# A hybrid recurrent decoder step on one core: zeros by ScalarE, VectorE's PSUM copies, one engine per bank in the planner, and a split start of the DeltaNet projection

## The chip, the core and the metric

The kernel runs on one core of a Trainium2 chip. The core has five instruction streams: TensorE (PE in the profile, PEld for its weight loads), VectorE (DVE), ScalarE (ACT), GpSimd (POOL) and SyncE (SP), which here only issues DMAs. The metric is the device time of one execution in microseconds.

## The reference

One step of a four-layer decoder trunk runs for a prompt of 256 tokens and for a sample group of 8 sequences with 4 new tokens each. That makes 288 token columns, all in fp32 with D_MODEL = 1024. Layers 0 and 3 use an S5 mixer, layer 1 an RG-LRU, layer 2 a gated DeltaNet. A causal ConvFFN follows each.

```python
def rmsnorm(x, g):
    return x * lax.rsqrt(jnp.mean(x * x, axis=-1, keepdims=True) + RMS_EPS) * g

def s5_mixer(x, h0_re, h0_im, w_in, a_re, a_im, log_dt, b_re, b_im, c_re, c_im, d, w_glu):
    u = x @ w_in
    lam = lax.complex(a_re, a_im);  dt = jnp.exp(log_dt)[:, None]
    a_bar = jnp.exp(lam * dt)
    b_bar = ((a_bar - 1.0) / lam)[..., None] * lax.complex(b_re, b_im)
    ...            # h[t] = a_bar * h[t-1] + b_bar u[t], y = Re(c h), in 64 groups of 16 channels
    y = jax.nn.gelu(y + d * u)
    val, gate = jnp.split(y @ w_glu, 2, axis=-1)
    return val * jax.nn.sigmoid(gate), h_last

for i in range(4):
    h = rmsnorm(x, mixer_gain[i]);  x = x + mixer[i % 3](h)
    h = rmsnorm(x, ffn_gain[i])
    up, conv = causal_dwconv(h @ w_up[i]);  x = x + (silu(gate half) * value half) @ w_down[i]
y = rmsnorm(x, final_gain)
```

The DeltaNet projects h to queries, keys, values, gates z and 16 scalars (beta and decay for 8 heads), convolves q, k and v, and runs a chunked delta rule. All recurrent states are returned too.

## The kernel before

The residual x stays in SBUF, transposed: 8 blocks of 128 channels by 288 tokens. Each projection is tiled into output tiles of 128 channels. A tile is summed over its k-blocks in one PSUM bank (names ps or px).

**Two ways to multiply.** In the split form the weight unit wr (128x1024, loaded by a DMA on SP's queue) is cut into a rounded part wh (ScalarE) and a rest wl (VectorE or GpSimd). The operand is cut likewise into xh and xl. Each k-block then takes three products of the type fp32r: xh·wh, xl·wh and xh·wl. In the whole form there is no cut, and each k-block is one plain fp32 product, which the trace shows as two records. `whole(u)` (L493) says which unit takes which: before, all of s5_in and gdn_in and a part of lru_in are whole. `WHOLE` lists the norms whose operand xh is written in plain fp32; the others write xh and xl.

**The planner.** The kernel is written as generators, which a small scheduler runs in Python when the program is built (class `Net`, with `tick`, `spawn`, `after`, `mark`). Each engine's wrapper (class `Eng`) books a price for every instruction, and `Trace.free` says from when its operands may be touched. The order that comes out of this is fixed in the program. A generator spawned with a lower rank goes first. All instructions are emitted by one wrapper line (L235 before, L243 after), so that rows are told apart by tile names.

**The stages in order.** s5_in, s5_glu, FFN 0, lru_in, lru_out, FFN 1, gdn_in, gdn_out, FFN 2, s5_in, s5_glu, FFN 3, final norm. Each begins when the residuals (x) before it are summed.

**The S5 layer** (`s5`, L1179). For each of 8 blocks m of 8 groups, `prep` (L1280) builds the state's input weights. TensorE writes them to a bank through vx and ci, VectorE scales 32 columns into wt, and 96 columns are copied to wt by whichever engine the planner thinks is free. `chain` (L1367) then takes the two-bank product pv, multiplies it by the phase tables e_r and e_i on VectorE (x, y), copies the sample part to fin on ScalarE, writes the decay tile r4 on ScalarE with a zero column by GpSimd, scans on VectorE (x<-r,x), builds the chunk states ss (its first columns copied from h0 on GpSimd, a column of the end state copied to fin on GpSimd) and forms the output y. vx and ca are block-diagonal tiles; their zeros are written once per layer by GpSimd. The tables (`s5_tables`, L1027: ex, er, dt, ang, rho, ...) are small VectorE operations on 32 columns. For layer 3 they run within FFN 2, as its `beside`.

**The end** (`final`, L2274). Eight squares are summed over channels by products with a column of ones. rsqrt is a chain of 11 VectorE operations on 128x3. The result is spread over a diagonal (dg), broadcast by a product with ones (busy), copied to SBUF (rstd), and eight operations write y, each with a DMA of its own.

Fills: when the planner thinks that TensorE would idle, it emits products on a constant tile (busy) into a warm bank.

Of the kernel before, what the change touches and what calls it, by code (L numbers as in the profile page):

```python
# [16 lines left out]
P = 128  # L17
D = 1024
# [19 lines left out]
OE, CE = 0, 'a'  # L38
PRS, DB, TH, BI = 1, 4, 8, 0.0
SR, SS = (0, 2, 1), (1000.0, 2000.0)  # L40
WHOLE = (0, 4, 6)
# [62 lines left out]
class Trace:  # L104
# [11 lines left out]
    def free(self, kind, writes, reads):  # L116

        at = 0.0
        for ts, w in ((writes, True), (reads, False)):
            for t in ts:  # L120
                a, b, c, d = self.region(t)
                for (e, f, g, h), wrote, by, end in self.tiles.get(self.place.get(t.name, t.name), ()):
                    if (w or wrote) and end + SEEN[by][kind] > at and a < f and e < b and c < h and g < d:
                        at = end + SEEN[by][kind]
        return at
# [21 lines left out]
class Eng:  # L147
# [56 lines left out]
    def __getattr__(self, name):  # L204
        f = getattr(self.real, name)

        def call(*a, **k):
            out = k["out"] if "out" in k else a[0]
            n = math.prod(out.shape[1:])
            args = [b for b in (*a, *k.values()) if hasattr(b, "ap")]  # L210
            writes = [b for b in args if b is out or b is k.get("accum_out")]
            reads = [b for b in args if not any(b is w for w in writes)]
            free = self.net.trace.free(self.kind, writes, reads)
            if self.kind == "pe":
                end = self.product(name, a[1], a[2], k.get("tile_position"), free)
            else:
                fn = a[2] if len(a) > 2 else None
                if self.kind == "a" and any(fn in s for s in SETS) and fn not in self.table:

                    self.t += 1283.0  # L220
                    self.table = next(s for s in SETS if fn in s)
                c = self.price(n, name)
                if self.kind in "va" and n > 1 and any(math.prod(b.shape[1:]) == 1 for b in reads):
                    c += self.POINTER[self.kind]
                streams = sum(b.space != PSUM and math.prod(b.shape[1:]) > 1 for b in reads)
                shared = self.kind == "g" and streams > 0 or self.kind == "v" and (
                    streams > 1 or streams == 1 and name in SINGLE and out.space != PSUM
                )
# [64 lines left out]
class Net:  # L293
# [121 lines left out]
    def tick(self):  # L415
        self.ahead()
        while self.warm and self.pe.cool():

            bank, alone = self.warm[-1]
# [52 lines left out]

    def scale(self, out, in_, s, kinds="va"):
# [243 lines left out]
    def ffn(self, li, gi, beside=()):  # L717
# [5 lines left out]
        with ExitStack() as es:  # L723
# [455 lines left out]
    def s5(self, li, gi, tables=None):  # L1179
# [7 lines left out]
        with ExitStack() as es:  # L1187
# [33 lines left out]
            def doubles():  # L1221
# [4 lines left out]
                self.warm.insert(0, (big[0][:, 1], True))  # L1226
# [3 lines left out]
                del self.warm[0]  # L1230
# [23 lines left out]
            for _, v in vxs.free + cas.free:  # L1254
                G.memset(v, 0.0)
# [24 lines left out]
            def prep(m):  # L1280
# [34 lines left out]
                self.copy(w[:, :96], ps[:, :96])  # L1315
# [51 lines left out]
            def chain(m, ps):  # L1367
# [24 lines left out]
                A.activation(fin[:, :, q0:q1, :NB], pv[:, :, :, :NB], AF.Copy)  # L1392
# [20 lines left out]
                G.tensor_copy(ssm[:, :, :, 0:NB], h0[:, :, q0:q1, :])  # L1413
# [7 lines left out]
                G.tensor_copy(fin[:, :, q0:q1, NB], ssm[:, :, :, NCK])  # L1421
# [83 lines left out]
            G.memset(cas.free[-1][1], 0.0)  # L1505
# [23 lines left out]
    def gdn(self, gi):  # L1529
# [6 lines left out]
        with ExitStack() as es:  # L1536
# [61 lines left out]

            def scalars():
                yield from self.after("gw")  # L1600
                ps = yield from self.banks.get()
                for k in range(KD):
                    yield from self.after(("x", g0, k))
                    PE.matmul(ps[0:16, :T], wab[:, k, :], self.xh[:, k, :], start=k == 0, stop=k == KD - 1)
                    if k % 2:
                        yield PE
                yield
# [633 lines left out]
            for m, ps in zip(tiles, self.gemm("gdn_in", tiles[:start], KD, self.xh, self.xl, self.xready(g0))):  # L2241
                self.spawn(fns[m // NH](m % NH, ps), rank=rk(m))
            for m in tiles[start:]:
                self.spawn(fns[m // NH](m % NH, *self.gemm("gdn_in", [m], KD, self.xh, self.xl)), rank=rk(m))
# [29 lines left out]
    def final(self):  # L2274
        self.drain()
        self.spawn(self.norm_rstd(8))
        self.drain()
        yp = self.ctx.enter_context(self.tc.tile_pool(name="yp", bufs=4))
        for m in range(KD):
            y = yp.tile([P, T], F32, name="y", tag="y")  # L2280
            self.v.scalar_tensor_tensor(
                y, self.x[:, m, :], self.gains[:, 8, m : m + 1], self.rstd, op0=ALU.mult, op1=ALU.mult
            )
            self.dma(self.o["y"][:, m, :], y)
# [192 lines left out]
```

## Time and profile before

| | us |
|---|---|
| three runs | 1572.19, 1572.41, 1567.34; median 1572.19 |
| the profiled execution, its own time | 1569.18 |
| its span | 1567.4 |
| PE / DVE / ACT / POOL busy in the span | 1503.2 / 1280.4 / 807.0 / 360.8 |
| s5_in, s5_glu (layer 0) | 7.1 to 184.1 |
| FFN 0 | 184.1 to 396.0 |
| gdn_in | 728.8 to 937.1 |
| FFN 2's down projection | 1110.9 to 1184.9 |
| s5_in, s5_glu (layer 3) | 1184.9 to 1340.7 |
| final norm and y | 1552.2 to 1567.4 |

TensorE is busy for 96% of the span, so the stages in which it is not are of interest. [...] A timeline row gives the start, the busy time, the engine and the operation, and in brackets how long the engine had been idle and what released it. Starts tell the pace of TensorE, since products overlap.

### The profile page before, as it was taken

The page shows a single profiled execution, that of the slowest core. Times are in us where ns is not written, and L with a number is a line of the kernel's source. Part 1 is how long each engine was busy: PE and PEld are TensorE (multiplying, and loading weights), DVE is VectorE, ACT ScalarE, POOL GpSimd, SP SyncE. Part 2 cuts the span into 40 slices and gives each one's busy share as a digit, 9 for nine tenths or more (in the row PEclk, how much of TensorE's full clock was granted, in tenths as well). Part 3 has the DMA queues.
Part 4 walks back from the last instruction along what each step waited for, and adds up shares of the span by engine and source line. Part 5 has one row for each costly group of instructions (what it writes and reads, how often), then busy time and mean ns, then how long its engine had stood idle before and what let it go on. Part 6 is the DMA issues. An engine that isn't in the chain of part 4 may idle for free. (4 is left out here: it accounts for less than half of the span.)

```text
span 1567.4 us, 32702 instructions
## 1 busy us (share of the span) xinstructions
PE 1503.2 (96%) x12527; PEld 1390.6 (89%) x12527; DVE 1280.4 (82%) x2884; ACT 807.0 (51%) x1594; POOL 360.8 (23%) x734
## 2 busy tenths in 40 slices
PE   6689999999999999999999999999999899999996
PEld 5568999999988999998777779999997779999996
DVE  8898799975868899943887677999997967899944
ACT  3475466654574566642543334666444635566631
POOL 2021044520211245400111010444201310245400
PEclk8799999999999999999999999999999999999998
DMA  4422444455425544554322536544545235544552
GB/s 156 113 88 87 161 177 162 163 174 172 174 81 152 195 168 164 163 174 149 122 95 70 195 101 212 178 171 161 156 149 157 55 105 169 166 169 163 161 176 68
DMA packets 84909, 230.05 MB, mean 147 GB/s; under 512 B 19088, under 2 KB 28688, under 8 KB 84752
## 3 DMA queue, kind: packets, MB, share of 16 engines
q1 hardware_dynamic: 84752, 227.96, 44.5%
q8 instruction: 98, 1.61, 0.4%
q14 instruction: 59, 0.48, 0.1%
HBM read 216.94 MB, written 10.99 MB: 145 GB/s over the span
## 5 line engine op out<-in xcount | busy, mean ns | idle before, releaser
L235 DVE TENSOR_TENSOR wl<-wr,wh 128x1024 fp32r<-128x1024 f32 (+2 forms) x338 | 397.9, 1179 | 132.1 <-PE px L235 36.5
L235 ACT ACTIVATE wh<-wr 128x1024 fp32r<-128x1024 f32 (+2 forms) x338 | 344.9, 1023 | 208.2 <-PE ps L235 77.7
L235 DVE SCALAR_TENSOR_TENSOR cv<-ext,par,cv 128x304 f32<-128x304 f32 (+1 forms) x420 | 258.2, 615 | 11.3 <-ACT cv L235 3.3
L235 PE MATMUL px<-xh,wh 128*128 128x288 f32 x776 | 231.0, 298 | 0.0
L235 PE MATMUL px<-xl,wh 128*128 128x288 f32 x776 | 228.9, 295 | 0.0
L235 PE MATMUL px<-xh,wl 128*128 128x288 f32 x776 | 228.7, 295 | 0.0
L235 PE MATMUL ps<-xh,wh 128*128 128x288 f32 x712 | 210.6, 296 | 0.0
L235 PE MATMUL ps<-xl,wh 128*128 128x288 f32 x712 | 210.0, 295 | 0.0
L235 PE MATMUL ps<-xh,wl 128*128 128x288 f32 x712 | 209.9, 295 | 0.0
L235 POOL TENSOR_TENSOR pr<-cv,cv 128x32 f32<-128x32 f32 (+1 forms) x156 | 165.9, 1083 | 58.8 <-DVE cv L235 55.3
L235 POOL COPY sto<-ext 128x16 f32<-128x16 f32 (+3 forms) x379 | 103.4, 275 | 310.8 <-DVE ext L235 287.2
L235 ACT ACTIVATE cv<-ext,par 128x304 f32<-128x304 f32 (+1 forms) x210 | 130.6, 626 | 85.1 <-DVE ext L235 70.7
L235 PE MATMUL ps<-gl,wh 128*128 128x288 f32 x568 | 169.7, 299 | 3.6 <-DVE gl L235 3.3
L235 PE MATMUL ps<-gh,wh 128*128 128x288 f32 x568 | 169.5, 298 | 2.6 <-ACT gh L235 2.5
L235 PE MATMUL ps<-gh,wl 128*128 128x288 f32 x568 | 169.0, 298 | 0.3 <-DVE wl L235 0.3
L235 PE MATMUL px<-gh,wh 128*128 128x288 f32 x536 | 159.1, 297 | 2.4 <-DVE gh L235 2.4
L235 PE MATMUL px<-gh,wl 128*128 128x288 f32 x536 | 158.8, 296 | 0.3 <-DVE wl L235 0.3
L235 PE MATMUL px<-gl,wh 128*128 128x288 f32 x536 | 159.0, 297 | 0.0
L235 PEld LDWEIGHTS px<-xh,wh 128*128 128x128 f32 x776 | 145.9, 188 | 0.8
L235 PEld LDWEIGHTS px<-xl,wh 128*128 128x128 f32 x776 | 145.9, 188 | 0.8
L235 PEld LDWEIGHTS px<-xh,wl 128*128 128x128 f32 x776 | 145.8, 188 | 0.0
L235 PE MATMUL ps<-xh,wr 128*128 128x288 f32 x416 | 125.4, 436 | 12.1 <-DMA wr<-s_in 7.1
(547 smaller groups left out, 3055.0 us busy)
## 6 DMA issues: line engine op xcount, KB each, us to landing
wr<-ffn_up SPq DMA_DIRECT2D x176, 512.0 KB, 3.5
wr<-ffn_down SPq DMA_DIRECT2D x64, 448.0 KB, 3.3
wr<-s_glu SPq DMA_DIRECT2D x32, 512.0 KB, 3.9
wr<-ffn_down SPq DMA_DIRECT2D x32, 512.0 KB, 3.5
wr<-gdn_in SPq DMA_DIRECT2D x32, 512.0 KB, 3.5
wr<-lru_in SPq DMA_DIRECT2D x20, 512.0 KB, 3.2
wr<-s_in SPq DMA_DIRECT2D x16, 512.0 KB, 3.8
wr<-lru_out SPq DMA_DIRECT2D x16, 320.0 KB, 2.9
```

The source lines that it names most:

```text
L235: return f(*a, **k)
```

## The change

1. **DeltaNet projection.** The first eight tiles (the keys, `NP3 = 8`) and the 16 scalars take the split form; the norm before it therefore writes xh and xl. From the ninth tile on the whole form is used as before, on a plain fp32 operand xf that ScalarE writes anew into the buffer of xl (`operand`).
2. **FFN 2.** The tables of layer 3 are spawned after the first down tile, at rank 1, in place of ahead of it.
3. **The final norm.** Sums over squares go into three banks, the earlier blocks' before the last is there, with fills between. The reciprocal root is broadcast by three fp32 products against the identity, y is read straight from PSUM and written to one tile, and five DMAs take it out in place of eight.
4. **S5.** Zeros of vx, ca and sx come from ScalarE. The 96 columns of wt and the sample part fin are copied by VectorE alone. r4's zero column is written once per buffer, outside the loop. The copies ss<-h0 and fin<-ss go from GpSimd to ScalarE. Two warm banks are offered in place of one.
[...]

```diff
-WHOLE = (0, 4, 6)
+WHOLE = (0, 6)
+RB = 1
+NP3 = 8
+NK = 4, 10
@@ Trace.free
-                    if (w or wrote) and end + SEEN[by][kind] > at and a < f and e < b and c < h and g < d:
+                    late = end + SEEN[by][kind]
+                    if t.space == PSUM and by != kind:
+                        if late > at and c // 512 <= (h - 1) // 512 and g // 512 <= (d - 1) // 512:
+                            at = late
+                    elif (w or wrote) and late > at and a < f and e < b and c < h and g < d:
@@ Eng
-                shared = self.kind == "g" and streams > 0 or ...
+                shared = self.kind == "g" and (streams > 0 or name == "memset") or ...
@@ Net
+    def zero(self, t):
+        ...
+        self.act.activation(t, a.to_broadcast(list(t.shape)), AF.Copy, scale=0.0)
@@ whole
-        return name.startswith(("s5_in", "gdn_in")) or name == "lru_in" and m >= KL
+        return name.startswith("s5_in") or name == "gdn_in" and m >= NP3 or name == "lru_in" and m >= KL
@@ ffn
-            for g in beside:
-                self.spawn(g)
...
                 if m == 0:
                     self.dma(self.o["ffn_st"][li], sto)
+                    for g in beside:
+                        self.spawn(g, rank=RB)
@@ s5
             for _, v in vxs.free + cas.free:
-                G.memset(v, 0.0)
+                self.zero(v.rearrange("p i q t c -> p (i q t c)"))
+            for _, r in r4s.free:
+                G.memset(r[:, :, :, 0], 0.0)
...
-                self.copy(w[:, :96], ps[:, :96])
+                V.tensor_copy(w[:, :96], ps[:, :96])
...
-                A.activation(fin[:, :, q0:q1, :NB], pv[:, :, :, :NB], AF.Copy)
+                V.tensor_copy(fin[:, :, q0:q1, :NB], pv[:, :, :, :NB])
...
-                A.activation(r4, s.rho4[:, q0:q1].unsqueeze(1).unsqueeze(3).to_broadcast(X), AF.Copy)
-                yield
-                G.memset(r4[:, :, :, 0], 0.0)
+                A.activation(r4[:, :, :, 1:], rho.to_broadcast([P, 2, 4, NP - 1]), AF.Copy)
...
-                G.tensor_copy(ssm[:, :, :, 0:NB], h0[:, :, q0:q1, :])
+                self.copy(ssm[:, :, :, 0:NB], h0[:, :, q0:q1, :], CE)
...
-                G.tensor_copy(fin[:, :, q0:q1, NB], ssm[:, :, :, NCK])
+                self.copy(fin[:, :, q0:q1, NB], ssm[:, :, :, NCK], CE)
@@ gdn
+                for k in range(KD):
+                    for i, (w, x) in enumerate(((wah, self.xh), (wah, self.xl), (wal, self.xh))):
+                        PE.matmul(ps[0:16, :T], w[:, k, :], x[:, k, :], ...)
...
+                if m == NP3:
+                    while not self.marked("gx"):
+                        self.idle()
+                    x2 = self.xs.tile([P, KD, T], F32, name="xf", tag="xl"), None
+                    self.spawn(operand(x2[0]), rank=-1)
@@ final
+            for i, b in enumerate((*BLK[:2], slice(0, NS))):
+                PE.matmul(ps[:, b], r[:, i : i + 1].to_broadcast([P, P]), self.ident[:, :n], start=True, stop=True)
+            for m in range(KD):
+                V.scalar_tensor_tensor(
+                    y[:, m, :], self.x[:, m, :], self.gains[:, 8, m : m + 1], ps[:, :T], op0=ALU.mult, op1=ALU.mult
+                )
+                if m not in (2, 4, 6):
+                    self.dma(self.o["y"][:, e : m + 1, :], y[:, e : m + 1, :])
```

**TensorE at the start of gdn_in**, before: the first tile sums in ps_72, the scalars (wab) in px_1686, the second tile in ps_73; `dg,busy` broadcasts the norm's reciprocal root.

```order
L235 MATMUL px_1685<-busy,sm_96 128x1
L235 MATMUL ps_72<-xh,wr 128x288 x4
L235 MATMUL px_1686<-xh,wab 16x288 x2
L235 MATMUL ps_73<-xh,wr 128x288
...
L235 MATMUL ps_75<-dg,busy 128x288
```

The same place after, with the scalars in ps_72 and the tile in px_1718:

```order
L243 MATMUL ps_72<-xh,wh 16x288
L243 MATMUL ps_72<-xl,wh 16x288
L243 MATMUL ps_72<-xh,wl 16x288
...
L243 MATMUL px_1718<-xh,wh 128x288
L243 MATMUL px_1718<-xl,wh 128x288
L243 MATMUL px_1718<-xh,wl 128x288
L243 MATMUL ps_74<-dg,busy 128x288
```

Each whole product on xh and wr has become a triple on xh, xl, wh and wl; the norm's broadcast keeps its place.

**VectorE at the start of FFN 2's down projection**, before: cuts wl of the coming weights, the tables (er, dt) and the gate's rest gl, which the last k-block of the first down tile needs.

```order
L235 SCALAR_TENSOR_TENSOR er<-ek,ex 128x32
L235 SCALAR_TENSOR_TENSOR er<-ek,er 128x32
L235 TENSOR_SCALAR dt<-er 128x32
L235 SCALAR_TENSOR_TENSOR cv_10713<-ext_10711,par,cv_10713 128x304 x2
L235 TENSOR_TENSOR wl<-wr,wh 128x896
L235 SCALAR_TENSOR_TENSOR dt<-dt,er 128x32 x7
L235 SCALAR_TENSOR_TENSOR dt<-dt,es 128x32
L235 TENSOR_TENSOR gl<-pr_10719,gh 128x288
```

The same place after:

```order
L243 SCALAR_TENSOR_TENSOR cv_10918<-ext_10916,par,cv_10918 128x304 x2
L243 TENSOR_TENSOR wl<-wr,wh 128x896
L243 TENSOR_TENSOR pr_10924<-cv_10917,cv_10918 128x32
L243 TENSOR_TENSOR pr_10924<-cv_10917,cv_10918 128x256
L243 CAST gh<-pr_10924 128x288
L243 TENSOR_TENSOR gl<-pr_10924,gh 128x288
L243 TENSOR_TENSOR wl<-wr,wh 128x1024
L243 TENSOR_TENSOR x<-x,px_1718 128x288
L243 TENSOR_SCALAR ex<-sc 128x32
```

The tables (ex and what follows) now stand behind the last gate and the first residual, and the last gate product pr and its cast gh are VectorE's too.

**ScalarE in s5_in of layer 0**, before, from the first chain on:

```order
L235 ACTIVATE vx_145<-pa_162 64x16x16 x4
L235 ACTIVATE fin<-px_634 128x2x4x8
L235 ACTIVATE r_172<-rho_107 128x512
L235 ACTIVATE ci_137<-ci_137 128x128
L235 ACTIVATE wt_141<-px_635 128x96
L235 ACTIVATE wh<-wr 128x1024
```

The same place after, and what follows when the first chunk states are there:

```order
L243 ACTIVATE vx_145<-pa_162 64x16x16 x4
L243 ACTIVATE r_172<-rho_107 128x8x63
L243 ACTIVATE ci_137<-ci_137 128x128
L243 ACTIVATE wh<-wr 128x1024
...
L243 ACTIVATE ss_146<-h_127 128x8x8
L243 ACTIVATE vx_144<-pa_164 64x16x16 x4
L243 ACTIVATE fin<-ss_146 128x2x4
L243 ACTIVATE r_172<-rho_107 128x8x63
L243 ACTIVATE ci_136<-ci_136 128x128
```

fin<-px and wt no longer stand in ScalarE's row ahead of ci; fin<-ss, which waits for VectorE's ss, does later on.

## Rows read from the trace of the kernel before

**Rows 1.** Windows by stage: stretch, length, busy PE, PEld, DVE, ACT, POOL, clock, DMA.

```profile
659.00:728.80 69.80, 69.80 (x530) 69.80 (x529) 34.37 (x47) 28.75 (x40) 2.40 (x4) 1.00 0.54 167
728.80:937.10 208.30, 206.43 (x1875) 153.66 (x1873) 158.79 (x506) 86.32 (x283) 23.58 (x61) 1.00 0.37 121
1110.90:1184.90 74.00, 72.20 (x530) 71.56 (x530) 67.31 (x211) 28.87 (x41) 4.11 (x7) 0.98 0.52 157
```

**Rows 2.** Timeline of PE in gdn_in: start, busy time, operation, count.

```profile
918.55 2.11 PE L235 MATMUL px<-xh,wr 128*128 128x288 f32 x8
920.49 2.10 PE L235 MATMUL ps<-xh,wr 128*128 128x288 f32 x8
```

**Rows 3.** Groups by form in gdn_in: operation, count, busy time, mean ns of one.

```profile
L235 ACT ACTIVATE wh<-wr 128x1024 fp32r<-128x1024 f32 x4 | 4.2, 1058 | 2.0 <-DMA wr<-gdn_out 2.0
L235 DVE TENSOR_TENSOR wl<-wr,wh 128x1024 fp32r<-128x1024 f32 x2 | 2.5, 1225 | 1.6 <-ACT wh L235 1.6
```

**Rows 4.** Timeline of PE, first down tile of FFN 2.

```profile
1120.36 0.40 PE L235 MATMUL ps<-gh,wh 128*128 128x288 f32 x1 [0.90 <-ACT gh L235]
1121.66 0.40 PE L235 MATMUL ps<-gl,wh 128*128 128x288 f32 x1 [0.90 <-DVE gl L235]
```

**Rows 5.** Timeline of DVE at the same place.

```profile
1118.94 2.07 DVE L235 SCALAR_TENSOR_TENSOR dt<-dt,er 128x32 f32<-128x32 f32 x7
```

**Rows 6.** Window of PE alone behind that: length, busy PE, clock, DMA.

```profile
1122.00:1126.50 4.50, 4.50 (x25) 0.62 0.58 191
```

**Rows 7.** Timeline of DVE in the final norm.

```profile
1556.91 0.42 DVE L235 TENSOR_TENSOR dg<-ident,rsr 128x256 f32<-128x256 f32 x1
...
1559.48 1.80 DVE L235 SCALAR_TENSOR_TENSOR y<-x,gains,rstd 128x288 f32<-128x288 f32 x4
...
1561.92 2.03 DVE L235 SCALAR_TENSOR_TENSOR y<-x,gains,rstd 128x288 f32<-128x288 f32 x4 [0.64 <-DMA o_y<-y]
```

**Rows 8.** Windows of the S5 layers up to the last gate, columns as in rows 1.

```profile
5.36:141.10 135.74, 109.90 (x1335) 86.61 (x1335) 121.17 (x348) 64.53 (x152) 21.29 (x38) 0.87 0.31 97
1184.90:1297.20 112.30, 102.40 (x1352) 82.06 (x1350) 88.26 (x182) 56.92 (x133) 22.92 (x42) 0.95 0.32 95
```

**Rows 9.** Timeline of the start: POOL, DVE, ACT.

```profile
3.17 1.85 POOL L235 MEMSET ca<- 128x1024 f32 x2
...
2.46 2.90 DVE L235 TENSOR_SCALAR ex<-sc 128x32 f32<-128x32 f32 x1 [2.46 <-DMA sc<-s_sc]
...
5.72 0.44 ACT L235 ACTIVATE acc<-x 128x288 f32<-128x288 f32 x1 [3.70 <-DMA x<-x]
```

**Rows 10.** Timeline in s5_in of layer 0: ACT, PE, DVE.

```profile
68.18 0.22 ACT L235 ACTIVATE fin<-px 128x64 f32<-128x64 f32 x1 [4.10 <-DVE x L235]
...
69.31 1.10 PE L235 MATMUL px<-vx,ci 128*32 128x128 f32 x14 [5.03 <-ACT ci L235]
...
76.17 1.29 DVE L235 TENSOR_TENSOR x<-px,ee 128x512 f32<-128x512 f32 x2 [3.46 <-PE px L235]
```

**Rows 11.** The tile wt, both layers: durations min/median/max in ns, and who waited for it (us, times).

```profile
L235 ACT ACTIVATE wt<-px x4: 251/252/253, 36.5 to 1211.4; 128x96 f32<-128x96 f32 x4
...
L235 DVE COPY wt<-px x2: 249/250/250, 89.7 to 1257.3; 128x96 f32<-128x96 f32 x2
...
  ACT wt L235: 23.5, 9
```

**Rows 12.** The tile fin, both layers: what its writers' engines waited for (us, times).

```profile
  DVE x L235: 41.1, 15
  DVE ss L235: 29.1, 11
```

**Rows 13.** Timeline in s5_in of layer 3: POOL, PE.

```profile
1238.78 5.48 POOL L235 COPY ss<-h 128x64 f32<-128x64 f32 x1
...
1244.31 0.46 PE L235 MATMUL px<-ss,ca 128*32 128x72 f32 x16 [2.19 <-DVE wt L235]
```

**Rows 14.** Window behind it, columns as in rows 1.

```profile
1245.90:1252.70 6.80, 6.80 (x68) 6.21 (x57) 5.55 (x10) 4.82 (x11) 2.95 (x4) 0.50 0.01 4
```

More of the change, by code (lines that the diff above doesn't have):

```diff
@@ L417, in tick @@
         while self.warm and self.pe.cool():
-            bank, alone = self.warm[-1]
+            at = [w for w in self.warm if self.trace.free("pe", [w[0]], []) <= self.now]
+            if not at:
+                break
+            bank, alone = at[-1]
             self.pe.matmul(
@@ L471, in tt @@
         self.best(math.prod(out.shape[1:])).tensor_tensor(out, a, b, op=op)
+    def zero(self, t):
+        n = len(t.shape) - 1
+        a = self.ident[:, :1]
+        for _ in range(n - 1):
+            a = a.unsqueeze(2)
+        self.act.activation(t, a.to_broadcast(list(t.shape)), AF.Copy, scale=0.0)
     def scale(self, out, in_, s, kinds="va"):
@@ L1225, in doubles @@
                 twos.put(*big)
-                self.warm.insert(0, (big[0][:, 1], True))
+                self.warm[:0] = [(big[0][:, i], True) for i in range(2)]
                 self.banks.put(*small)
@@ L1229, in doubles @@
                 yield from twos.get(PRS)
-                del self.warm[0]
+                del self.warm[:2]
                 if small:
@@ L1504, in s5 @@
             vts.free.append((0.0, more[:, 1024:2048].rearrange("p (q i n) -> p q i n", q=4, i=2)))
-            G.memset(cas.free[-1][1], 0.0)
+            self.zero(more[:, :1024])
             while not self.marked(*(("sv", li, m) for m in range(GW))):
@@ L1597, in pack, with operand @@
                     V.tensor_copy(pk[32 * h : 32 * h + 32, dst, :], src[0:32, 2, h::4])
+            def operand(xf):
+                for m in range(KD):
+                    A.activation(xf[:, m, :], self.x[:, m, :], AF.Copy, scale=self.gains[:, g0, m : m + 1])
+                    self.mark(("xf", m))
+                    if m % 2:
+                        yield
+                self.mark("xf")
             def scalars():
                 yield from self.after("gw")
+                wah, wal = (w.rearrange("p (k c) -> p k c", k=KD) for w in (wh, wl))
+                self.copy(wah, wab)
+                yield
+                V.tensor_tensor(wal, wab, f32(wah), op=ALU.subtract)
+                yield
                 ps = yield from self.banks.get()
@@ L1603, in scalars @@
                     yield from self.after(("x", g0, k))
-                    PE.matmul(ps[0:16, :T], wab[:, k, :], self.xh[:, k, :], start=k == 0, stop=k == KD - 1)
+                    for i, (w, x) in enumerate(((wah, self.xh), (wah, self.xl), (wal, self.xh))):
+                        PE.matmul(ps[0:16, :T], w[:, k, :], x[:, k, :], start=k + i == 0, stop=k == KD - 1 and i == 2)
                     if k % 2:
                         yield PE
+                self.mark("gx")
                 yield
@@ L2274, in final, with norm @@
     def final(self):
-        self.drain()
[L2276 to L2284, printed above, removed]
+        V, PE = self.v, self.pe
+        y = self.xs.tile([P, KD, T], F32, name="y", tag="xh")
+        def norm():
+            yield from self.after(("n", 8, KD - 2))
+            pss = yield from self.banks.get(3)
+            spare = yield from self.banks.get()
+            for m in (KD - 2, KD - 1):
+                yield from self.after(("n", 8, m))
+                for ps, b in zip(pss, BLK):
+                    sq = self.acc if m < KD - 1 else self.last
+                    PE.matmul(ps[:, :1], sq[:, b], self.ones[:, :1], start=m < KD - 1, stop=m == KD - 1)
+                for _ in range(NK[m - KD + 2]):
+                    PE.matmul(
+                        spare[:, : 2 * P].rearrange("p (a c) -> p a c", a=2), self.busy,
+                        self.busy.unsqueeze(1).to_broadcast([P, 2, P]), start=True, stop=True,
+                    )
+            v = self.work.tile([P, 3], F32, name="nv", tag="nv")
+            for i, ps in enumerate(pss):
+                V.tensor_scalar(v[:, i : i + 1], ps[:, :1], 1.0 / D, EPS, op0=ALU.mult, op1=ALU.add)
+            r = self.rsqrt(v, [P, 3], "nr")
+            ps = pss[0]
+            for i, b in enumerate((*BLK[:2], slice(0, NS))):
+                n = b.stop - b.start
+                PE.matmul(ps[:, b], r[:, i : i + 1].to_broadcast([P, P]), self.ident[:, :n], start=True, stop=True)
+            e = 0
+            for m in range(KD):
+                V.scalar_tensor_tensor(
+                    y[:, m, :], self.x[:, m, :], self.gains[:, 8, m : m + 1], ps[:, :T], op0=ALU.mult, op1=ALU.mult
+                )
+                if m not in (2, 4, 6):
+                    self.dma(self.o["y"][:, e : m + 1, :], y[:, e : m + 1, :])
+                    e = m + 1
+        self.spawn(norm())
+        self.drain()
 def wtiles(w):
```

9 lines of the change are left out of this document (6 added, 3 removed).

## The prediction

> **What bounds the kernel now.** I read the windows by stage first. The FFN stages have TensorE busy for their whole length: the down projection of FFN 1 takes 69.80 us with 69.80 of PE [rows 1]. Nothing can be gained there but by fewer products. Its 528 products give the pace of the split form: 69.80 / 528 = 0.1322 us. The DeltaNet projection is bound by TensorE too: 206.43 of 208.30 us busy, with VectorE at 158.79 [rows 1]. There the form of the products sets the time. The down projection of FFN 2 has the same products as that of FFN 1 and takes 74.00 us, 4.2 more, with VectorE at 67.31 in place of 34.37 [rows 1]. The timelines then tell of the rest. The S5 layers are the two places where TensorE waits for the other engines. Up to the last gate, VectorE is busy for 121.17 of 135.74 us in layer 0, and for 88.26 of 112.30 in layer 3 [rows 8]. So layer 0 is nearly VectorE's length, and layer 3 is a chain with gaps on every engine. The end is a chain of small operations on one engine at a time.
>
> **The change part by part.** The sum is made against the profiled execution, 1569.18 us. This lies between the fastest run (1567.34) and the median (1572.19).
>
> *The DeltaNet projection.* In the whole form eight records take 920.49 − 918.55 = 1.94 us [rows 2], thus 0.2425 for a record and 0.485 for a k-block of two. In the split form a k-block takes 3 × 0.1322 = 0.397. Eight tiles of eight k-blocks change: 64 × 0.088 = 5.6 us less, and the scalars' eight k-blocks give 0.7 more. What is added is eight cuts wh at 1.06 us on ScalarE and eight wl at 1.22 on VectorE [rows 3], with eight operand rests xl, each of fewer elements than a wl. These are under 20 us on VectorE, which has 49 us free in this stage [rows 1], and they lie beside TensorE's 25 us for those tiles. At the ninth tile ScalarE writes xf anew in eight operations, each at most 1.06 by its cuts. TensorE needs only the first of them to go on. It then pays some 0.5 us, or at most 8.5 if it waited for all. I take −6, with −6.4 and +2 as ends.
>
> [...] The rows show 132.2 ns in a full stage, and the sum goes by these.
>
> *FFN 2's down projection.* TensorE waited 0.90 us for gh and 0.90 for gl [rows 4], while VectorE did seven table operations dt in 2.07 us ahead of gl [rows 5]. Behind that the clock was at 0.62 of full over 4.5 us [rows 6], which is 1.7 us lost. Fills take up the remainder of the 4.2 us. The change puts the tables behind the first residual and the last gate. What is late next is VectorE itself: the tables are about 67.31 − 34.37 = 33 us, and seven eighths of the stage (61 us) have to hold them and seven eighths of the other 34. That is 63 in 61, so that up to 2 us may come back at the start of layer 3. I take −3.5, from −4.2 to 0.
>
> *The end.* From the diagonal dg to the first y there are 2.57 us: two operations, a product at half clock and a copy [rows 7]. After, three small products on the identity stand in their place, with no VectorE operation between. I put them at 1.0 us. The wait of 0.64 for an output buffer [rows 7] goes. The statistics' scale becomes three operations in place of one, 0.4 more by the 0.3 us of a small operation [rows 5]. Earlier sums and fewer DMAs I count at nothing: the last DMA is of one block as before. −1.6 − 0.6 + 0.4 is about −2, with −4 and +1 as ends.
>
> *S5, layer 0.* VectorE's first operation ex took 2.90 us, from 2.46 on, beside GpSimd's zeros [rows 9]. Seven operations of the same width took 2.07 elsewhere [rows 5], so that 2.6 us go with the zeros. ScalarE pays for these with four operations of about 1.06 [rows 3]: they end about half a microsecond behind the time when x came (5.72) [rows 9], which only TensorE's first product sees. VectorE gets seven copies wt and eight copies fin, at most 0.25 us each [rows 11]: up to 3.8, of which I take 3. On the other side stands ScalarE's queue. fin, which waits for VectorE's x, held up r and ci behind it: 4.10 us of ScalarE, 5.03 of TensorE, and then 3.46 of VectorE [rows 10]. Over both layers ScalarE waited 41.1 us at fin [rows 12] and 23.5 at wt [rows 11]. In the new order neither stands ahead of ci. VectorE's gaps up to the last gate are 135.74 − 121.17 = 14.6 us [rows 8]; I take the 3.46 and about one more: −2.6 + 3 − 4.4 = −4. If two thirds of the gaps went it would be −9; if none went and the head start was lost, +3.
>
> *S5, layer 3.* GpSimd's copy ss<-h0 took 5.48 us beside a busy VectorE; TensorE waited 2.19 [rows 13], and then its clock was 0.50 over 6.8 us [rows 14], which loses 3.4. The copy goes to ScalarE, so that 5.6 us are to be had. VectorE gets 4 copies wt and 8 fin, up to 3 us, half of it under its 24 us of gaps [rows 8]: −5.6 + 1.6 = −4. The ends are −9 (more of TensorE's idle goes, as in layer 0) and +3 (the work counts in full and nothing goes).
>
> The other layers keep their order; I count them at 0, between −1.5 and +1.5. Sum: −6 − 3.5 − 2 − 4 − 4 = −19.5, so 1549.7 for an execution like the profiled one. For the median I add half of the 3.0 us between that and the median before: about 1551.
>
> **The rivals.**
>
> *Copies only change engines.* A copy wt takes 250 ns on VectorE and 252 on ScalarE [rows 11], so that moving it saves no work. ScalarE's waits would then have been slack, and the waits for ss only move to its queue. What speaks for it is that 64 us of ScalarE's waits at fin and wt [rows 11, 12] came out as few waits of TensorE. Against it speak the 5.03 and the 3.46 of rows 10. The S5 layers then give 0: −11.5, about 1559. [...]
>
> *More goes than I count.* The S5 layers give −9 each, at the ends above: −29.5, about 1541.
>
> *ScalarE's queue becomes the bound (slower).* fin<-ss, which GpSimd had, now stands in ScalarE's row ahead of r and ci. On GpSimd these copies waited 29.1 us for VectorE's ss [rows 12]. On ScalarE each such wait holds up ci, hence TensorE, hence VectorE's x. If all of it came on the path, with VectorE's 4.6 us of copies: −11.5 + 29.1 + 4.6 = +22, about 1593. Slower by 4.7 us than the median before (0.3%, about what a measurement of this kernel can tell from no change) needs the S5 layers to lose 16 us, so some two fifths of those 29.1 on the path beside the copies. Against it: the planner orders by when it believes ss to be there, and ScalarE is half idle there.
>
> *The split start doesn't do what it says.* If TensorE, at the change of operands, waits for all of xf (+8.5 in place of 0.5), the stage is 2 us longer, not 6 shorter: about 1559, and about 1567 with the first rival. Against it: xf is marked block by block.
>
> **How the numbers follow.** The forecast has 0.50 (1545 to 1556). Copies that only change engines: 0.22, faster still. More than I count: 0.15. The split that fails: 0.02, faster. S5 losses of 7 to 16 us, which leave the whole within 0.3%: 0.07. Beyond that: 0.04. So faster is 0.89, same 0.07 and slower 0.04. For the range, the lower end is the second rival's 1541, and one for the DeltaNet's end; the upper end takes in the first rival with FFN 2 and the end at their poorer bounds (1559 + 3.5 + 2): 1540 to 1565.
>
> **What would show it.** In the windows of after, the DeltaNet projection should be 202 us long with no wait of TensorE over 1 us at its ninth tile, and FFN 2's down projection 70 to 71 with the clock at 1.00. From the first y to the last there should be no gap, and the last x to the end should be 13 us. In layer 0, ex should last under 0.5 us, and "ACT fin <- DVE x" should be gone from the waits. If "ACT fin <- DVE ss" stands in its place with tens of microseconds, and TensorE waits for ci behind it, the third rival is at work. If the S5 stages keep their lengths, the first is. The forecast is wrong above all if layer 0 turns out longer by VectorE's copies while its gaps remain.

## The result, and the profile after

The changed kernel takes 1546.58 us (median of four runs, 1542.24 to 1547.11) where the kernel before takes 1572.26 (four runs): a ratio of 0.9838 with a 95% interval of 0.9812 to 0.9864. That is 25.7 us faster. The profiled execution has a span of 1545.2 us, 22.2 less than the one before.

Where the 22.2 us went, by stages: the start of a stage is the start of its first product. "Again" is a second profile of the changed kernel, from the experiments.

| stage | before | after | again | forecast |
|---|---|---|---|---|
| S5, layer 0 (s5_in and s5_glu) | 177.0 | 169.2 | 168.4 | −4 |
| RG-LRU (in and out) | 121.5 | 124.5 | 120.8 | 0 |
| DeltaNet (in and out) | 240.6 | 234.7 | 235.9 | −6 |
| FFN 2, down | 74.0 | 70.6 | 70.6 | −3.5 |
| S5, layer 3 | 155.8 | 151.7 | 153.2 | −4 |
| FFN 3, down, to the end | 85.2 | 81.8 | 81.8 | −2 |
| all other FFN stages | 706.1 | 706.0 | 706.0 | 0 |

First the windows of after that answer to [rows 1], for the DeltaNet projection and FFN 2's down projection (stretch, length, then busy time of PE, PEld, DVE, ACT and POOL, the clock granted to TensorE as a share of full speed, DMA share and GB/s):

```profile
723.56:926.28 202.72, 200.06 (x1955) 157.34 (x1954) 163.68 (x513) 91.05 (x286) 24.95 (x62) 1.00 0.37 121
1099.76:1170.35 70.59, 70.08 (x531) 69.85 (x530) 67.83 (x213) 28.43 (x40) 4.20 (x6) 1.00 0.56 165
```

The projection is 5.6 us shorter and TensorE has 6.4 us less to do; VectorE has 4.9 more, which makes 163.7 of the 202.7. The down projection has its 70 us, though VectorE is as busy as before: the same tables, at another place.

VectorE's first operation, and layer 0 from there to the last gate, answer to [rows 8, 9]:

```profile
2.48 0.23 DVE L243 TENSOR_SCALAR ex<-sc 128x32 f32<-128x32 f32 x1 [2.48 <-DMA sc<-s_sc]
```

```profile
2.45:133.00 130.55, 108.38 (x1359) 84.29 (x1359) 124.78 (x363) 70.16 (x157) 10.15 (x11) 0.95 0.35 107
```

ex takes 0.23 us where it took 2.90. The last gate comes at about 133.0, where before it came at 141.1. Of these 130.6 us VectorE is busy for 124.8. Before, from the end of ex on, it was 121.2 of 135.7: its work has grown by 3.4 us, ex itself not counted, and its gaps have shrunk from 14.6 to 5.8. VectorE's waits in that stretch (us in total, times, longest) tell which gaps went. Two of the waits before:

```profile
DVE gl L235 <- ACT gh L235: 4.2, 3, 2.2
DVE x L235 <- PE px L235: 3.5, 1, 3.5
```

After, neither is left, and the 1.0 us of waits at wt is gone too: 8.7 us together. Those behind g and sx or ca on ScalarE (2.3 and 1.2 before, 2.4 and 1.1 after) have stayed.

The end, on VectorE and TensorE, answers to [rows 7]:

```profile
1533.48 0.45 DVE L243 TENSOR_TENSOR x<-x,px 128x288 f32<-128x288 f32 x1 [6.11 <-PE px L243]
1534.94 0.16 DVE L243 TENSOR_SCALAR nv<-px 128x1 f32<-128x1 f32 x1 [1.01 <-PE px L243]
...
1537.56 0.16 DVE L243 SCALAR_TENSOR_TENSOR rsr<-rst,rsr 128x3 f32<-128x3 f32 x1
1538.67 3.49 DVE L243 SCALAR_TENSOR_TENSOR y<-x,gains,px 128x288 f32<-128x288 f32 x8 [0.95 <-PE px L243]
```

Eight y follow each other without a gap, and only the products on the identity stand between the last rsr and the first y.

### The profile page after: what moved, and what is told of

It is laid out like the page before. It is cut to its first block, busy times and chain, and to the rows that moved or that the text cites. A ratio compares the mean times of both kernels' runs of the same rounds, so it can differ in the third digit from the quotient of the medians.

```text
span 1545.2 us, 32927 instructions
## 1 busy us (share of the span) xinstructions
PE 1493.2 (97%) x12636; PEld 1390.8 (90%) x12636; DVE 1290.6 (84%) x2926; ACT 827.0 (54%) x1616; POOL 328.1 (21%) x678
## 4 chain that ended last, share of the span: by engine, by line
PE 59%; DVE 7%; ACT 1%; issue 1%; DMA 0%; SPq 0%; DVEq 0%; ACTq 0%
PE px L243 30%; PE ps L243 29%; DVE x L243 1%; DVE cv L243 1%; DVE wl L243 1%; DVE pa L243 1%; DVE yy L243 0%; DVE s L243 0%; ACT vx L243 0%; DVE fh L243 0%; DVE rst L243 0%; DVE mt L243 0%; ACT ca L243 0%; DVE oa L243 0%; DVE pk L243 0%
## 5 line engine op out<-in xcount | busy, mean ns | idle before, releaser
L243 DVE TENSOR_TENSOR wl<-wr,wh 128x1024 fp32r<-128x1024 f32 (+2 forms) x346 | 407.9, 1180 | 136.7 <-PE ps L243 40.0
L243 ACT ACTIVATE wh<-wr 128x1024 fp32r<-128x1024 f32 (+2 forms) x346 | 353.4, 1024 | 230.1 <-PE px L243 84.5
L243 PE MATMUL ps<-xh,wh 128*128 128x288 f32 x776 | 230.8, 297 | 0.0
L243 PE MATMUL ps<-xl,wh 128*128 128x288 f32 x776 | 228.9, 295 | 0.0
L243 PE MATMUL ps<-xh,wl 128*128 128x288 f32 x776 | 228.7, 295 | 0.0
L243 POOL COPY sto<-ext 128x16 f32<-128x16 f32 (+2 forms) x375 | 101.0, 271 | 327.9 <-DVE ext L243 304.5
L243 PEld LDWEIGHTS ps<-xl,wh 128*128 128x128 f32 x776 | 145.2, 187 | 1.1
```

## The experiments

Seven kernels undo one part each; they are compared with the changed kernel by stages, since a stage's time in the profile is told to some tenths while whole runs differ by several us. The first run is the changed kernel itself. Four small parts were not undone singly: r4's zero column, the second warm bank, the planner's `shared` for a GpSimd memset, and the rule that a fill goes only to a bank that is free.

**The changed kernel again.**

> The changed kernel once more, to see how far one profiled execution differs from the next. In the first one the RG-LRU's output projection took 38.2 us where before had 35.3, with the granted clock at 0.74 over 10 us of it. If that comes from the new order (waits for gl in a fixed place), it is 38 us again. If it is chance in when the clock falls (the rival), it is 35.3, and the execution is some 3 to 5 us shorter, as one of the four runs was. All other stages within 0.5 us of the first profile.

Measured: 1545.1 us (1544.59 to 1545.96). The RG-LRU took 120.8 us, its output projection 34.5. So the 38.2 of the first profile was chance. The window of the first profile in that projection, and that of the second in which the same products run:

```profile
482.00:492.00 10.00, 10.00 (x59) 10.00 (x59) 4.90 (x9) 4.59 (x8) 0.00 (x0) 0.74 0.45 135
```

```profile
480.40:488.20 7.80, 7.80 (x61) 7.80 (x60) 5.26 (x9) 4.48 (x8) 0.00 (x0) 1.00 0.63 173
```

In the first the granted clock was 0.74 on average over 10 us, behind waits for the gate's rest gl of 2.0 us in all; in the second it stayed at 1.00, with 1.0 us of the same waits. The same program is 3.7 us apart there. The waits alone do not decide it: before had 1.9 us of them in this stage and kept a clock of 1.00. Layer 3 differed by 1.5, the output of the DeltaNet by 1.2, layer 0 by 0.8, where the expectation had allowed 0.5. That is the measure for what follows: a stage with waits is known to some 1.5 us, and one with a fall of the clock to 4.

**The DeltaNet projection wholly in plain fp32.**

```diff
-WHOLE = (0, 6)
+WHOLE = (0, 4, 6)
-NP3 = 8
+NP3 = 0
...                             # no cut of wab into wah and wal
-                for i, (w, x) in enumerate(((wah, self.xh), (wah, self.xl), (wal, self.xh))):
-                    PE.matmul(ps[0:16, :T], w[:, k, :], x[:, k, :], ...)
+                PE.matmul(ps[0:16, :T], wab[:, k, :], self.xh[:, k, :], ...)
```

> The changed kernel with the DeltaNet projection wholly in plain fp32 as before (no split tiles, scalars in plain fp32, no new operand). By my theory (64 k-blocks at 0.485 in place of 0.397 us, and 0.7 for the scalars, less 0.5 for the change of operand) its stage is back from 202.7 to 208.3 us, and the whole is 5.5 to 6 us slower than the changed kernel. By the rival (the stage gained through the planner's new rule for banks, not through the split) it stays near 203.

Measured: 1551.22 us, against 1545.1 beside it on the same chip: 6.1 slower. Its window of the projection:

```profile
720.02:930.45 210.43, 208.08 (x1874) 154.30 (x1873) 161.56 (x508) 83.80 (x271) 21.68 (x64) 0.99 0.38 120
```

210.4 in place of 202.7, so 7.7 us; with the output projection, 242.6 in place of 234.7 to 235.9, so 6.7 to 7.9. TensorE's busy time carries it: 208.1 in place of 200.1. The split is the cause; the rival falls. The stage is even 2 us longer than before's plain form (240.6). Of these, 1.7 are TensorE's busy time in the projection: 208.1 us for 1874 products at a mean clock of 0.99, where before had 206.4 for 1875 at 1.00 [rows 1]. With as many products, I put these 1.7 down to the clock.

**The tables ahead of FFN 2's down projection.**

```diff
+            for g in beside:
+                self.spawn(g)
             self.fresh(gi)
...
-                    for g in beside:
-                        self.spawn(g, rank=RB)
```

> The changed kernel with the tables of layer 3 spawned ahead of the down projection of FFN 2, as before. By my theory the waits for gh and gl at the end of the first down tile and the half clock behind them return: the stage goes from 70.6 to 74, and the S5 layer behind it gets shorter by at most 1 us. By the rival (in the new order pr and gh are VectorE's there, so that no wait comes of the tables) it stays at 70 to 71.

Measured: 1546.12 us. The stage took 72.8, so 2.2 of the 3.4 came back. Its window, and TensorE's waits in it (us in total, times, longest):

```profile
1095.34:1168.13 72.79, 70.95 (x534) 70.32 (x533) 67.29 (x211) 28.65 (x41) 4.09 (x7) 1.00 0.55 161
```

```profile
PE px L243 <- DVE gl L243: 0.9, 1, 0.9
PE px L243 <- ACT gh L243: 0.7, 1, 0.7
```

The two waits of [rows 4] are back, 0.9 and 0.7 in place of 0.9 and 0.9. The clock, at 0.62 in [rows 6], stayed at 1.00 here; that is the missing third. Layer 3 behind it took 151.7, as in the first profile of the changed kernel (153.2 in the second).

**The end as before.**

```diff
-    def final(self):
-        ...                     # three banks, products on the identity, one tile y, five DMAs
+    def final(self):
+        self.drain()
+        self.spawn(self.norm_rstd(8))
+        ...                     # dg, rstd, eight tiles y with a DMA each
```

> The changed kernel with the final norm and the output as before. From the end of the last down projection to the end 15.2 us were needed before and 11.8 after. By my theory the 3.4 us come back in full, 81.8 to 85.2 from the start of that projection; nothing else moves, as nothing follows. By the rival (part of the gain is the clock at the end, or the planner's rule) under 2 us come back.

Measured: 1545.75 us; 84.6 from the last down projection's start in place of 81.8, so 2.8 of the 3.4 come back. On its VectorE the diagonal and the first y stand as far apart as before, and the wait for an output buffer is there:

```profile
1534.64 0.42 DVE L243 TENSOR_TENSOR dg<-ident,rsr 128x256 f32<-128x256 f32 x1
...
1537.22 1.81 DVE L243 SCALAR_TENSOR_TENSOR y<-x,gains,rstd 128x288 f32<-128x288 f32 x4
1539.65 2.03 DVE L243 SCALAR_TENSOR_TENSOR y<-x,gains,rstd 128x288 f32<-128x288 f32 x4 [0.63 <-DMA o_y<-y]
```

These three runs did not move the whole by as much as their stages (6.1, 1.0 and 0.7 us). The smaller two lie within the spread of the runs, so that these parts are shown by their stages alone.

**The S5 layers, one part undone at a time.** Four more kernels.

```diff
 # copies: wt and fin
-                V.tensor_copy(w[:, :96], ps[:, :96])
+                self.copy(w[:, :96], ps[:, :96])
-                V.tensor_copy(fin[:, :, q0:q1, :NB], pv[:, :, :, :NB])
+                A.activation(fin[:, :, q0:q1, :NB], pv[:, :, :, :NB], AF.Copy)
 # zeros
-                self.zero(v.rearrange("p i q t c -> p (i q t c)"))
+                G.memset(v, 0.0)
...                             # sx likewise
 # ss and the end state
-                self.copy(ssm[:, :, :, 0:NB], h0[:, :, q0:q1, :], CE)
+                G.tensor_copy(ssm[:, :, :, 0:NB], h0[:, :, q0:q1, :])
...                             # fin<-ss likewise
 # the planner's rule for banks: the body of Trace.free as before
```

> The changed kernel, with only the copies undone: the 96 columns of wt by the engine that the planner thinks free, the sample part fin by ScalarE, as before. Layer 0 up to the last gate had 14.6 us of gaps on VectorE before and 5.8 after. Theory 1 (ScalarE's queue made the gaps: fin and wt wait there for VectorE and hold up ci): the gaps come back to 11 to 15 us while VectorE has some 3 us less work, and the layer (7 to 176 us) gets 3 to 6 us longer. Theory 2 (the planner's rule for banks made the order better, the copies only move 3 us of work): the layer gets shorter by 0 to 3 us, or stays.

> The changed kernel with the zeros of vx, ca and sx by GpSimd again. Theory (VectorE's first operation is held up by GpSimd's memsets and all that VectorE does in layer 0 shifts with it): ex takes about 2.9 us again in place of 0.23, and layer 0 gets 2 to 3 us longer; layer 3, where the zeros lie in the middle of other work, changes by less than 1. Rival (the head start is lost again in a later wait): ex takes 2.9, but the layer stays within 0.7.

> The changed kernel with the copies ss<-h0 and fin<-ss on GpSimd again. Theory (GpSimd's small copies beside a busy VectorE take several us and hold up ss, so TensorE in layer 3): copies of several us show again among GpSimd's, and layer 3 (151.7 us) gets 2 to 5 longer. Rival (they were late before because of the order, not by the engine; on GpSimd they don't wait in ScalarE's queue for VectorE's ss): layer 3 within 1 us, and layer 0 shorter by up to 3, as ScalarE's 5.7 us of waits for ss go.

> The changed kernel with the planner's old rule for operands in PSUM (overlap of the very elements; an engine may be booked on a bank that another holds). Theory 1 (the copies and zeros made the S5 gains): both S5 layers within 2 us of 169.2 and 151.7. Theory 2 (the rule made them): layer 0 gets 3 to 8 us longer, and layer 3 2 to 4. In the DeltaNet projection the rule should then show too, by up to 2 us.

Measured:

| undone | whole | ratio to before | layer 0 | layer 3 | DeltaNet |
|---|---|---|---|---|---|
| nothing (again) | 1545.1 | 0.984 (0.9824 to 0.9855) | 168.4 | 153.2 | 235.9 |
| copies | 1541.24 | 0.9812 (0.9794 to 0.983) | 171.2 | 145.9 | 234.9 |
| zeros | 1541.16 | 0.981 (0.9795 to 0.9825) | 174.8 | 148.9 | 230.2 |
| ss | 1540.5 | 0.9799 (0.9779 to 0.9819) | 169.2 | 150.7 | 233.6 |
| rule for banks | 1542.61 | 0.9824 (0.9803 to 0.9845) | 168.4 | 149.2 | 234.5 |

As whole kernels, the four are 2.5 to 4.6 us below the changed kernel, which ran on another chip (before took 1571.0 us on the one and 1571.1 on the other). The interval of ss alone lies clear of the second measurement of the changed kernel (0.9824 to 0.9855), and all overlap that of the first (0.9812 to 0.9864). So no run shows that one of these four parts pays in the whole while the others are in place; what each does is read by stages.

In layer 0 two parts pay: the copies 2.8 us and the zeros 6.4. The copies of ss (0.8) and the rule (nothing) move it by no more than the changed kernel's two profiles differ. With the zeros undone, VectorE begins as before (the first row); with the copies undone, ScalarE waits at fin and wt as before (us, times, longest):

```profile
2.50 2.90 DVE L243 TENSOR_SCALAR ex<-sc 128x32 f32<-128x32 f32 x1 [2.50 <-DMA sc<-s_sc]
```

```profile
ACT fin L243 <- DVE x L243: 24.3, 7, 5.5
ACT wt L243 <- DVE wt L243: 15.6, 3, 6.4
```

VectorE's busy time to the last gate is then 123.4 of 132.6 us, gaps of 9.2 in place of 5.2, with 1.3 us less work. Theory 1 of the copies holds there, just under its lower end (2.8 where 3 to 6 were expected): they take 4.0 us of gaps away and cost 1.3 of work. The zeros took more than expected: undone, VectorE has 123.8 us of work in the 133.1 from the end of ex to the last gate, so gaps of 9.3 in place of 5.2, on top of the 2.7 of the start. TensorE's clock in that stretch is 0.91 in place of 0.95; whether this has a part in the gaps is not shown.

In layer 3 every one of the four, undone, made the layer shorter: by 2.5 to 7.3 us against the second profile, by 1.0 to 5.8 against the first (151.7). Here the copies are the plainest case. The layer with ScalarE's copies, and ScalarE's waits at them, beside the layer of the changed kernel (windows as above):

```profile
1168.50:1314.50 146.00, 139.68 (x1672) 120.13 (x1671) 119.85 (x227) 84.77 (x189) 20.84 (x21) 1.00 0.41 127
```

```profile
ACT fin L243 <- DVE x L243: 21.2, 8, 5.7
...
ACT wt L243 <- DVE wt L243: 7.7, 4, 2.9
```

```profile
1167.00:1320.00 153.00, 143.50 (x1665) 122.62 (x1664) 121.89 (x242) 87.55 (x181) 4.89 (x14) 0.97 0.40 120
```

29 us of ScalarE's waits are there, and TensorE, whose gaps are 6.3 us in place of 9.5 and whose clock is at 1.00 in place of 0.97, is done 7 us earlier. So in layer 3 those waits are slack. Of the 7 us, 3.2 are gaps and 3.8 are busy time for as many products, which is the clock. With the rule for banks undone the gaps stay (9.7 us) and only the clock is better, so that its 4 us are the clock's alone (TensorE: stretch, length, busy, clock, DMA):

```profile
1166.91:1316.16 149.25, 139.51 (x1667) 1.00 0.42 124
```

Whether such a fall belongs to an order or to one execution, a single profile of each kernel does not tell. The DeltaNet column moves too: with the zeros undone, an edit that does not touch this projection, it took 199.2 us of the 230.2, with 2.7 us less work for TensorE than in the changed kernel. So the order is worth some us there as well. And with ss back on GpSimd, its copy ss<-h took up to 6.8 us somewhere (0.24 in the median), but in layer 3 at most 0.7: whether such a copy takes long where TensorE waits for it came with the order.

**One number of the planner.**

```diff
-    BASE = {"v": (68.0, 1.042), "a": (98.0, 0.833), "g": (150.0, 2.25)}
+    BASE = {"v": (68.0, 1.042), "a": (100.0, 0.833), "g": (150.0, 2.25)}
```

> The changed kernel with one number of the planner changed: the base price of a ScalarE operation is 100 ns in place of 98. No operation is added, dropped or given to another engine by it, but the order is planned anew. This measures how much of a stage's time is chance of the order. Theory 1 (the order is robust; what single edits moved by 3 to 7 us in the S5 layers is the edits' own): every stage within 1 us of the changed kernel. Theory 2 (every edit plans the rest anew, and that alone moves an S5 or RG-LRU stage by 2 to 5 us): layers 0 and 3 and lru_in move by that much, the FFN stages by nothing, and the whole by up to 5.

Measured: 1544.75 us; layer 0 168.1, layer 3 153.0, DeltaNet 235.7, RG-LRU 122.3. Against the second profile of the changed kernel the RG-LRU moved by 1.5 us, less than between the two profiles of one program, and everything else by less than 1. So theory 1 holds but for that stage, although VectorE's order differs in many places. This is one small edit; the 2.5 to 7.3 us in layer 3 are more than it moved.

**Copies undone in layer 3 alone, and 16 split tiles.**

```diff
-                V.tensor_copy(w[:, :96], ps[:, :96])
+                if li:
+                    self.copy(w[:, :96], ps[:, :96])
+                else:
+                    V.tensor_copy(w[:, :96], ps[:, :96])
...                             # fin likewise; for the second kernel also, tiles counted in their order:
-NP3 = 8
+NP3 = 16
```

> The changed kernel with the copies of wt and fin undone in layer 3 alone (ScalarE has fin, wt goes to a free engine); layer 0 has them on VectorE. With them undone in both layers, layer 0 was 2.8 us longer (171.2 in place of 168.4) and layer 3 was 7.3 shorter (145.9 in place of 153.2). Theory (VectorE's copies pay in layer 0, which VectorE bounds, and cost in layer 3, which they lengthen): layer 0 168.4, layer 3 146 to 148, the whole some 6 us under the changed kernel, 1539 or so. Rival (layer 3's gain came by chance of the order): layer 3 at 150 or more.

> As the kernel with the copies undone in layer 3 alone, and with 16 tiles of the DeltaNet projection split in place of 8 (the first 16 in their order). By the k-blocks (eight tiles more, 64 times 0.088) the stage goes from 202.7 to 197 while TensorE bounds it. VectorE has 163.7 of 202.8 us busy now and gets 8 cuts more of 1.22 us. Rival: VectorE and ScalarE, which in the second eight tiles have the delta rule's work too, become late, TensorE waits, and the stage stays over 201.

Measured for the first kernel: 1545.44 us; layer 0 168.9, layer 3 150.6. That is 1.1 to 2.6 us under the changed kernel's layer 3, far from the 145.9 with the copies undone in both layers. By its number the rival holds. TensorE's window of the layer tells more:

```profile
1170.25:1320.84 150.59, 143.34 (x1673) 0.97 0.41 123
```

Its gaps are 7.2 us, nearer to the 6.3 of the kernel with both undone than to the 9.5 of the changed kernel. Its busy time is 143.3, where it was 139.7 at a clock of 1.00 with both undone. So of the 4.7 us between these two kernels 3.7 are the clock's. My theory holds for 2 to 3 us of gaps, which went in both kernels with the copies on ScalarE, and fails for the remainder of the 7. Why the clock fell in the one and not in the other is open.

For the second: 1556.21 us, 10.8 slower than the first, from which it differs in the 16 alone. By the stages, the DeltaNet with its output lost 7.7 us (242.5), layer 3, which the 16 do not touch, lost 5.3 (155.9), and the RG-LRU gained 3.5. The projection:

```profile
720.31:928.44 208.13, 197.79 (x2008) 161.56 (x2007) 173.57 (x505) 99.31 (x293) 28.65 (x69) 0.98 0.37 118
```

TensorE has 2.3 us less to do than with eight tiles, but 10.3 us without work in place of 2.7. TensorE's longest waits there are for ScalarE's part of the delta rule (jk 2.1 us, mt 2.1, kq 1.6) and for its new operand xf (1.6). The rival was right: what is split in the second eight tiles competes with the delta rule's work on ScalarE and VectorE.

**The zeros alone, in the kernel before.**

```diff
-                G.memset(v, 0.0)
+                self.zero(v.rearrange("p i q t c -> p (i q t c)"))
...
-            G.memset(cas.free[-1][1], 0.0)
+            self.zero(more[:, :1024])
```

> The kernel before with the zeros of vx, ca and sx written by ScalarE, and nothing else of the change. Undoing the zeros in the changed kernel made layer 0 6 us longer (174.8 in place of 168.4). Theory 1 (VectorE's head start of 2.7 us is all that the zeros give by themselves; the remainder came of a new order): layer 0 gets 2 to 3.5 us shorter than before's 177.0, other stages within 1 us, the whole 2 to 4 shorter. Theory 2 (the memsets cost in the middle of the layer too): 5 to 7 shorter. Theory 3 (a head start is lost again in ScalarE's waits for fin and wt, which are still there): within 1 us of 177.0.

Measured: 1563.36 us, a ratio of 0.9952 (0.9933 to 0.997) to before. ex took 0.18 us. Layer 0 took 174.6, so 2.4 less: in this layer theory 1 holds, the head start and no more. It does not hold elsewhere. The whole got 6.7 us shorter where 2 to 4 were expected, and four stages that the edit should have left within 1 us moved by 1.3 to 1.6 (RG-LRU, DeltaNet and FFN 2's down projection shorter, layer 3 longer). Undone in the changed kernel the zeros cost 6.4 in layer 0; by themselves they bring 2.4. The remaining 4 came only together with the other parts; which of them was not taken apart.

## Why the prediction was right, and where its terms were off

The time lies 4.4 us under the forecast and inside its range. Term by term:

- **DeltaNet, −6.** The stage lost 5.6 us, 5.9 with its output, and undoing it costs 6.7 to 7.9, of which 1.7 are the clock's. TensorE's busy time fell by 6.4 us, which is what 64 k-blocks and the scalars were said to give. At the ninth tile there is no wait for xf among TensorE's waits. The 132.2 ns of the rows stands: 528 such products still take 69.81 us in FFN 1.
- **FFN 2, −3.5.** It was −3.4. When the tables were put back, the two waits came back and the fall of the clock, for which I had counted 1.7, did not: 1.2 of the 3.4 stayed away. It belonged to that order or that execution. That up to 2 us would be lost at the start of layer 3 did not show.
- **The end, −2.** It was −3.4, and the step that was mis-sized is what I counted at nothing. From the start of the last x to nv 1.46 us pass in place of 2.36 (x started at 1552.18, nv at 1554.54 in the trace of before), since only the last block's sums are left: 0.9. From the last y's end to the end of the span it is 3.1 in place of 3.5; but with the old end and its eight DMAs put back it was 2.8, so that this is not shown to be the DMAs' doing. Of the steps that I did price, the broadcast took 0.91 us (from 0.2 after the last rsr's start, where dg stood, to the first y) in place of 2.57, with the clock at 1.00 (1537.56 to 1538.67) in place of 0.50 (1556.91 to 1559.48 in the trace of before), the eight y 3.49 in place of 4.47, and nv 0.45 more, as put but for 0.3 more on y.
- **Layer 0, −4.** It was −7.8 and −8.6 in the two profiles. The head start (2.6) and the added work (3, measured 3.4) were right in size. The term that failed is the gaps: I let 4.4 of VectorE's 14.6 us go, and 8.8 went. Beside the 3.5 at x, which I counted, VectorE no longer waits 4.2 us for ScalarE's gate cast gh and 1.0 at wt. Of the three waits for gh before, one (1.45 us) came of a gh that stood behind fin in ScalarE's row, and the longest (2.20) of one behind four writes of ca. So fin's place in the queue accounts for a part of them only. Undoing one part at a time shows why a third was too little. The copies, undone, bring 4.0 us of gaps back, and the zeros 4.1, where I had let the zeros give their head start alone. A rival is left: TensorE's clock rose from 0.87 to 0.95 in this stretch, and its share in the gaps is not separated. With the copies undone, though, the gaps came back at a clock of 0.95.
- **Layer 3, −4.** The sum was right by its number (−4.1 and −2.6) and not by its reason, so that this is luck. The copy of 5.48 us on GpSimd and the half clock behind it [rows 13, 14] are gone, but with ss back on GpSimd no such copy returns in this layer, and it was shorter (150.7). TensorE's gaps, of which I took 2.2 us away, fell by 0.8 alone, from 10.3 to 9.5. The remainder is its busy time (145.6 before, 142.2 and 143.7 after), and the clock of the layer was 0.97 before, 0.98 and 0.97 after. With the same parts in place or one undone, layer 3 took 146 to 153 us, and up to 4 of these 7 are the clock's. My step read one event of one order as if it were the engine's price.
- **The first rival** (copies only change engines) is right for layer 3, where 29 us of ScalarE's waits cost TensorE no gap, and wrong for layer 0. "ACT fin <- DVE x" is gone, as foretold, but r, which comes next in ScalarE's queue, now waits for VectorE's x: 7.6 us in layer 0 and 6.2 in layer 3. **The third** (ScalarE's queue becomes the bound) didn't come: ScalarE waited 5.7 us for ss in layer 0 and 10.4 in layer 3, a little over half of the 29.1 that GpSimd had waited, but TensorE's waits for ci are only 3.8 and 2.5 us.

So the sum came out because DeltaNet, FFN 2 and, but for 1.4 us, the end were read from what bounds their stages. That it came so near is luck in part: layer 3's term was right for a wrong reason, and of the 4 that layer 0 gave beyond the forecast the profiled execution lost 3 again in the RG-LRU, most of it to the clock.

The kernel with ss and the end state copied by GpSimd measured the shortest of all: 1540.5 us, 0.9799 of before (0.9779 to 0.9819), where the changed kernel had 0.984 (0.9824 to 0.9855) on another chip. By the stages its gain is spread (DeltaNet −2.3, layer 3 −2.5, against layer 0 +0.8 and RG-LRU +1.0), so that I read it as a better order and no merit of GpSimd; no run separates the two.

## What to carry to other kernels

Price a change first in the stages that one engine bounds: there the count of instructions by their pace gave TensorE's time to a few tenths (6.3 us less foreseen, 6.4 found), while in stages that are chains across engines a single number of the sum was off by a factor of two or right for the wrong reason. A wait on an engine's queue is worth something only if the engine that bounds the stage waits behind it: look for the gap on that engine, not at the sum of the waits. Where a planner fixes the order, undo each part alone and read the stage. Compare TensorE's busy time and clock before you put a difference down to an engine or to the order. And treat a gain in a stage of many short waits as the order's until a second edit confirms it.

## What the runs showed of the hardware

- The same program ran the RG-LRU's output projection in 38.2 and in 34.5 us: in the one the granted clock was 0.74 over 10 us behind 2.0 us of waits, in the other 1.00 behind 1.0. One microsecond more of TensorE's waiting went with 3.7 us more of time. The amount of waiting does not settle whether the clock falls: with 1.9 us of these waits before, it was 1.00 and the stage took 35.3 us.
- In layer 3 TensorE's busy time for some 1670 products was 139.5 and 139.7 us at a mean clock of 1.00 (rule for banks undone, copies undone), and 141.9, 143.3 and 143.5 at 0.97 (ss undone, copies undone in layer 3 alone, the second profile of the changed kernel).
- A VectorE operation of 32 columns took 2.90 us beside GpSimd's memsets, in both profiled kernels where these stand at the start, and 0.18 to 0.23 in eleven others. A GpSimd copy of 64 columns took 0.24 us in the median and up to 6.8 in the kernel with ss back on GpSimd. Before, one took 5.48 us, and VectorE was busy for all of the 5.60 us from 1238.7 to 1244.3, in which it lies.
